# Weight sums of the column pairs by accumulating transfers, and retention steps one tick later

## The chip, the cores and the metric

The kernel runs on one core of a Trainium2 chip. The metric is the device time of one execution in microseconds (us), shown as the median of several runs. Each engine works through its own instruction list in order: TensorE (PE; its weight loads are shown as PEld), VectorE (DVE), ScalarE (ACT), GpSimd (POOL) and SyncE (SP), which issues the transfers. They meet through semaphores. A framework orders the instructions of each engine when the program is built, by dependencies, program order and its own estimates; on the chip the order is fixed.

## The reference

Two layers on x of 1024 tokens by 1024 channels, in float32. The change lies in the first, a retention layer:

```python
h = rmsnorm(x, g_pre)
proj = h @ w_in                                  # 1024 x 6144
q, k, v, gate = split(proj, [1024, 2048, 4096])
q = rope(q by 8 heads of 128); k = rope(k by 8 heads) * 128 ** -0.5; v by 8 heads of 256
# chunks of 64 tokens, per head:
scores = (q_i @ k_i.T) * inner_dec               # inside a chunk
cross  = (q_i @ R) * xi                          # from the state of the chunks before
R      = R * g_c + (k_i * zeta).T @ v_i
o = groupnorm(scores @ v_i + cross) * gn_gain
x = x + rmsnorm((silu(gate) * o) @ w_out, g_post)
```

The second layer is an attention over a shared compressed key and value (a gate projection, softmax over earlier chunks, an output projection); the change leaves its code as it is.

## The kernel before, in words

**Products.** A float32 matrix product is made of three matmuls on float32r parts: each operand is split into a high part (ScalarE, L238) and the rest (VectorE, L239), and `mm3` (L232 to L234) adds lo x hi, hi x lo and hi x hi. On top of that, the large products use Strassen's scheme in Winograd's form: seven half-size products in place of eight, with sums of blocks as operands.

**Column pairs.** In the first layer q, k and the gate are made in 16 column pairs, two for each of the eight heads: the q pair (columns of q and k) and the g pair (two gate columns). A pair is seven products, a to g (`pair`), each 12 matmuls of 128 x 512. The left operand of a product (its weights) is a "unit": half of a 128 x 1024 weight block, split in hi and lo. Three units are plain halves of the raw blocks r0 and r1 (`wraw`), four are sums T1 to T4 of such halves (`wsum`). Their making, in `make_sums`, is four subtractions on VectorE (L98, L99, L103, L104): T1 = r0 hi - r0 lo, T2 = r1 hi - T1, T3 = r1 hi - r0 hi, T4 = r1 lo - T2, where lo and hi are the column halves.

**When a unit is made.** `next` hands out a unit at the start of a product and prepares units until three are ready. It then sees to it that the pair after the next one is fetched: this falls at the start of product d of each pair, for the pair two further on. Buffers of 128 x 1024 come from one pool of 51 (`Heap`), first freed, first taken; a new writer waits for the last user of the buffer.

**Retention between the products.** After each product `tick` runs what is due of a list (`later`). When the last columns of q and k of a token half are there (half 1 after product f, half 0 after product g of the q pair), `rotate_a` applies the rope: two ScalarE copies of 64 x 1024 into xs (L656, L657), then three VectorE operations of 128 x 1024 (L660, L661, L662). From the end of the q pair, the four steps of each half are put on the list: scores (L693 transposes k, L699 multiplies q and k), values (the load `vt` is split), states (matmuls r<-v,z, then the state R is updated on VectorE, L755, and split), mix (matmuls r<-v,a and r<-r,q). The mix takes statistics on VectorE (L778, L779, L782), the power -0.5 on GpSimd (rg, L783) and nb on VectorE (L790). One product later ScalarE writes the normalized y (L793), and three products later TensorE transposes y (L810), VectorE multiplies by the gate (L813), and SyncE stores yT. The products at which these steps come are these numbers, counted from the end of the q pair:

```python
wait = (1, 2, 4, 6, 8, 9, 11, 13) if h < NH - 1 else (1, 2, 3, 5, 4, 6, 8, 10)
```

The first four are scores, values, states and mix of half 0, the others those of half 1. So half 0 comes in the head's g pair, half 1 in the q pair of the next head. The matmuls of these steps write PSUM tiles named r (four banks), those of the products tiles named acc (four banks).

Of the kernel before, what the change touches and what calls it, by code (L numbers as in the profile page):

```python
# [13 lines left out]
ALU = mybir.AluOpType  # L14
# [8 lines left out]
HALF = 512  # L23
HT = HALF // P
NT = S // P
NH = 8
# [6 lines left out]
class Heap:  # L33


    def __init__(self, pool, n):
        self.pool, self.n = pool, 0
        self.idle = deque(range(n))
        self.at = {}
# [13 lines left out]
class Units:  # L53
# [3 lines left out]

    def __init__(self, T, order, source, ahead, early=0):  # L60
        self.T, self.order, self.source, self.ahead, self.early = T, order, source, ahead, early
        self.at = self.n_fetched = 0
        self.pairs = list(dict.fromkeys(p for p, _ in order))
        self.raw, self.sums, self.made, self.left, self.ready = {}, {}, {}, {}, deque()

    def fetch(self):
        if self.n_fetched == len(self.pairs):
            return
        T, p = self.T, self.pairs[self.n_fetched]
        self.n_fetched += 1  # L70
        src, gains = self.source(p)
        self.raw[p] = [T.heap.get("wraw") for _ in range(2)]
        for j in range(2):
            r = self.raw[p][j]
            T.nc.sync.dma_start(r, src[j])
            if gains is not None:
                v = r.rearrange("p (n k c) -> p n k c", n=2, k=4)
                for k in range(4):
                    T.nc.scalar.activation(v[:, :, k, :], v[:, :, k, :], AF.Copy, scale=gains[:, 4 * j + k:4 * j + k + 1])  # L79
        self.left[p] = {"r0": 3, "r1": 5, "ta": 3, "tb": 3}  # L80

    def done(self, p, *names):
        left = self.left[p]
        for n in names:
            left[n] -= 1
            if not left[n]:
                self.T.heap.free(self.raw[p][int(n[1])] if n[0] == "r" else self.sums[p][n == "tb"])
# [110 lines left out]
class Trunk:  # L198
# [228 lines left out]
    def layer_a(self):  # L427
        nc, I, heap = self.nc, self.I, self.heap

        nc.scalar.activation(self.small([P, 1], "warm"), self.mhalf, AF.Silu)  # L430
        make_identity(nc, self.ident)
        self.X, A = {}, {}
        wide = WideUnits(self, NH // 4, lambda g, j, n, b: I["w_v"][g, j, n, b])
        rows = [[heap.get("xt") for _ in range(HT)] for _ in range(2)]
        for half in range(2):
            for t in range(HT):
                nc.sync.dma_start(rows[half][t], I["x"][half * HALF + t * P:half * HALF + (t + 1) * P, :])
                if half == 0 and t == 2:
                    wide.load(0)
            if half == 0:  # L440
                wide.load(1)
        self.first_rows(rows[0], A, wide)
        self.rows_norm(rows[1])
        for _ in self.rows_in(0, rows[0], A, ("A12",)):
            pass
        order = [(p, w) for p in range(2 * NH) for w in WINOGRAD]
        units = Units(self, order, lambda p: (I["w_in_a"][p], None), 3)
        self.values_a(wide, rows[1], A, units)
        sinks = [(h, kind) for h in range(NH) for kind in "qg"]
        self.heads = [{"h": h} for h in range(NH)]  # L450
        for p, (h, kind) in enumerate(sinks):
            if p == 2 * NH - 1:
                self.prepare_out_a()
            self.pair(units, getattr(self, "sink_" + kind)(h), over=p == 2 * NH - 1)
# [173 lines left out]
    def sink_q(self, h):  # L628

        st = self.heads[h]  # L630
        cb = {}

        def sink(i, j, bank, U):
            if i not in cb:
                cb[i] = [self.heap.get("qk"), 0]
            self.take(cb[i][0][:, j * HALF:(j + 1) * HALF], bank, U)
            cb[i][1] += 1
            if cb[i][1] == 2:
                st["qk", i] = cb[i][0]
                self.rotate_a(cb[i][0], i)  # L640
                if i == 0:
                    dm = st["dmask"] = self.small([P, P], "dm", bufs=2)
                    self.nc.sync.dma_start(dm, self.I["dmask"][:, h * P:(h + 1) * P])
                    wait = (1, 2, 4, 6, 8, 9, 11, 13) if h < NH - 1 else (1, 2, 3, 5, 4, 6, 8, 10)
                    steps = (self.ret_scores, self.ret_values, self.ret_states, self.ret_mix)
                    for n, (what, half) in zip(wait, [(w, i) for i in range(2) for w in steps]):
                        self.later(n, lambda what=what, half=half: what(st, half))
                    self.ret_load(st, 0)
                    self.later(wait[5] - 3, lambda: self.ret_load(st, 1))

        return sink
# [894 lines left out]
```

## Time and profile before

| | |
|---|---|
| median of 3 runs | 1268.6 us (1268.34 to 1268.72) |
| profiled execution | 1268.73 us |
| its span, first to last instruction | 1267.0 us |
| PE busy | 1240.5 us, 98% |
| DVE busy | 996.6 us, 79% |
| ACT busy | 639.6 us, 50% |
| POOL busy | 65.5 us, 5% |
| granted TensorE clock | 0.999 |

The profile is of one execution. A row of the groups reads: line, engine, operation, out<-in by the program's names, shape, count, then busy us, mean ns of one, and idle time of the engine before them with what ended it. A row of the timeline reads: start and duration in us, engine, line, operation, operands, count, and in brackets the idle time before it with its releaser. A matmul's duration includes the filling of the array, so matmuls overlap, and what one costs is the distance from its start to the next one's.

### The profile page before, as it was taken

How to read it: one execution, taken by the hardware profiler on the slowest of the kernel's cores; microseconds unless marked ns; L12 is line 12 of the kernel's file. 1: busy time of each engine (PE TensorE's matmuls, PEld its weight loads, DVE VectorE, ACT ScalarE, POOL GpSimd, SP SyncE). 2: the span in 40 equal slices, each digit the busy share in tenths (PEclk: the TensorE clock that was granted, in tenths of full speed). 3: DMA queues.
4: the chain of work that ended last, by engine and by line, in shares of the span. 5: the costliest groups of instructions: out<-in, count | busy, mean ns of one | idle time of the engine just before them, and what ended most of it. 6: DMA issues, size and time to landing. Idle time of an engine off the chain costs nothing. (4 is left out here: it accounts for less than half of the span.)

```text
span 1267.0 us, 17676 instructions
## 1 busy us (share of the span) xinstructions
PE 1240.5 (98%) x6568; PEld 1066.5 (84%) x6568; DVE 996.6 (79%) x1839; ACT 639.6 (50%) x1162; POOL 65.5 (5%) x86
## 2 busy tenths in 40 slices
PE   6999999999999999999999999999999999999997
PEld 5888878888888888888888789978898989898886
DVE  6888878898998998999966874675688788989622
ACT  7632125555564565565634875574445455456411
POOL 2000000000000000001000131200000000000000
PEclk9999999999999999999999999999999999999999
DMA  8248981232222322248663631124301020122321
GB/s 349 84 154 319 325 318 50 73 112 70 86 67 85 120 67 69 84 137 338 209 245 99 234 141 34 40 96 163 118 19 51 11 57 14 34 78 100 117 84 50
DMA packets 54166, 155.32 MB, mean 123 GB/s; under 512 B 6464, under 2 KB 15680, under 8 KB 54080
## 3 DMA queue, kind: packets, MB, share of 16 engines
q1 hardware_dynamic: 54080, 154.20, 34.9%
q8 instruction: 51, 0.84, 0.3%
q14 instruction: 35, 0.29, 0.1%
HBM read 113.28 MB, written 36.70 MB: 118 GB/s over the span
## 5 line engine op out<-in xcount | busy, mean ns | idle before, releaser
L232 PE MATMUL acc<-xhi,unit 128*128 128x512 f32 x560 | 220.6, 394 | 1.4 <-DVE unit L239 1.2
L233 PE MATMUL acc<-xlo,unit 128*128 128x512 f32 x560 | 219.2, 392 | 0.8 <-DVE xlo L239 0.8
L234 PE MATMUL acc<-xhi,unit 128*128 128x512 f32 x560 | 218.2, 390 | 0.0
L232 PEld LDWEIGHTS acc<-xhi,unit 128*128 128x128 f32 x560 | 105.3, 188 | 23.1 <-DVE unit L239 2.8
L234 PEld LDWEIGHTS acc<-xhi,unit 128*128 128x128 f32 x560 | 105.2, 188 | 21.7
L233 PEld LDWEIGHTS acc<-xlo,unit 128*128 128x128 f32 x560 | 105.4, 188 | 20.4 <-DVE xlo L239 1.1
L232 PE MATMUL acc<-vhi,xlo 128*128 128x512 f32 x224 | 89.3, 399 | 1.0 <-DVE xlo L239 1.0
L234 PE MATMUL acc<-vhi,xhi 128*128 128x512 f32 x224 | 88.4, 394 | 0.0
L233 PE MATMUL acc<-vlo,xhi 128*128 128x512 f32 x224 | 88.3, 394 | 0.0
L238 ACT ACTIVATE unit<-wsum 128x512 fp32r<-128x512 f32 x80 | 50.4, 631 | 59.9 <-PE acc L234 44.9
L1346 ACT ACTIVATE p<-S,nm 128x896 f32<-128x896 f32 (+3 forms) x64 | 47.4, 741 | 54.9 <-DVE nm L1343 50.2
L238 ACT ACTIVATE unit<-wraw 128x512 fp32r<-128x512 f32 x60 | 37.8, 630 | 53.6 <-issue 21.9
L238 ACT ACTIVATE pT<-r 128x512 fp32r<-128x512 f32 (+2 forms) x96 | 44.5, 489 | 37.8 <-PE r L1376 37.7
L238 ACT ACTIVATE vhi<-wv 128x1024 fp32r<-128x1024 f32 x28 | 29.3, 1060 | 64.4 <-PE acc L233 15.5
L239 DVE TENSOR_TENSOR unit<-wsum,unit 128x512 fp32r<-128x512 f32 x80 | 54.3, 684 | 8.5 <-ACT unit L238 8.2
L239 DVE TENSOR_TENSOR pT<-r,pT 128x512 fp32r<-128x512 f32 (+2 forms) x96 | 50.8, 549 | 4.8 <-ACT pT L238 4.5
L783 POOL TENSOR_TENSOR rg<-rg,mhalf 128x2 f32<-128x2 f32 x32 | 24.6, 769 | 548.2 <-DVE rg L782 528.0
L232 PEld LDWEIGHTS acc<-vhi,xlo 128*128 128x128 f32 x224 | 42.7, 191 | 10.1 <-DVE xlo L239 1.4
L232 PE MATMUL acc<-thi,slo 128*128 128x512 f32 x128 | 49.9, 393 | 0.6 <-DVE slo L239 0.6
L234 PEld LDWEIGHTS acc<-vhi,xhi 128*128 128x128 f32 x224 | 42.8, 191 | 9.1
L233 PEld LDWEIGHTS acc<-vlo,xhi 128*128 128x128 f32 x224 | 42.8, 191 | 8.7
L232 PE MATMUL acc<-whi,u 128*128 128x512 f32 x128 | 50.0, 391 | 0.0
(291 smaller groups left out, 3429.3 us busy)
## 6 DMA issues: line engine op xcount, KB each, us to landing
wraw<-in_w_in_a_dram SPq DMA_DIRECT2D x32, 512.0 KB, 4.1
wv<-in_w_v_dram SPq DMA_DIRECT2D x28, 512.0 KB, 6.3
wl<-in_w_out_a_dram SPq DMA_DIRECT2D x28, 512.0 KB, 6.0
yl<-yd SPq DMA_DIRECT2D x28, 512.0 KB, 4.8
vd<-vo SPq DMA_DIRECT2D x32, 256.0 KB, 2.9
td<-wl SPq DMA_DIRECT2D x16, 512.0 KB, 3.6
vt<-vd SPq DMA_DIRECT2D x16, 512.0 KB, 3.2
yd<-yT SPq DMA_DIRECT2D x16, 512.0 KB, 4.7
```

The source lines that it names most:

```text
L232: mm(ps, lhs[1], rhs[0], start=first, stop=False, skip_group_check=more)
L233: mm(ps, lhs[0], rhs[1], start=False, stop=False, skip_group_check=more)
L234: mm(ps, lhs[0], rhs[0], start=False, stop=last, skip_group_check=more)
L238: self.nc.scalar.activation(hi, src, AF.Copy)
L239: self.nc.vector.tensor_sub(lo, src, hi.bitcast(F32))
L783: nc.gpsimd.tensor_tensor(out=rg, in0=rg, in1=self.mhalf[:, 0:1].to_broadcast([P, 2]), op=ALU.pow)
L1346: nc.scalar.activation(p[:, :w].rearrange("p (a b) -> p a b", a=pieces), view, AF.Exp, bias=nm, accum_out=sm)
```

## The change

From the third column pair on, the four sums are no longer made by VectorE. At the fetch ScalarE writes -r0 into the buffer ta (128 x 1024) and -r1 hi into the second half of tb; SyncE copies r0 lo from DRAM into the first half of tb. Then three transfers issued by GpSimd add onto them: r0 hi and r1 hi onto the two halves of ta (T1 and T3), r1 lo onto the second half of tb, and, when all of these have landed, ta with its halves exchanged onto tb (T2 and T4). Besides, the retention steps of heads 0 to 6 come one product later.

```diff
@@ class Units
+    def __init__(self, T, order, source, ahead, early=0, queued=False):
...
+        self.queued = queued
@@ fetch
         self.left[p] = {"r0": 3, "r1": 5, "ta": 3, "tb": 3}
+        if self.queued and self.n_fetched > 2:
+            self.queue_sums(p, src)
+
+    def queue_sums(self, p, src):
+        T = self.T
+        nc = T.nc
+        ta, tb = self.sums[p] = [T.heap.get("wsum") for _ in range(2)]
+        lo, hi = slice(0, HALF), slice(HALF, 2 * HALF)
+        r0, r1 = self.raw[p]
+        two = lambda x: x.rearrange("p (j c) -> p j c", j=2)
+        onto = lambda o, i: nc.gpsimd.dma_start(o, i, accum_op=ALU.add)
+        nc.scalar.mul(ta, r0, -1.0)
+        nc.sync.dma_start(tb[:, lo], src[0][:, lo])
+        nc.scalar.mul(tb[:, hi], r1[:, hi], -1.0)
+        onto(two(ta), src.rearrange("j p c -> p j c")[:, :, hi])
+        onto(tb[:, hi], src[1][:, lo])
+        onto(two(tb), two(ta)[:, ::-1, :])
+        self.made[p] = {"T1", "T2", "T3", "T4"}
+        self.done(p, "r0", "r0", "r1", "r1", "r1", "ta", "tb")
@@ layer_a
-        units = Units(self, order, lambda p: (I["w_in_a"][p], None), 3)
+        units = Units(self, order, lambda p: (I["w_in_a"][p], None), 3, queued=True)
@@ sink_q
-                    wait = (1, 2, 4, 6, 8, 9, 11, 13) if h < NH - 1 else (1, 2, 3, 5, 4, 6, 8, 10)
+                    wait = (2, 3, 5, 7, 9, 10, 12, 14) if h < NH - 1 else (1, 2, 3, 5, 4, 6, 8, 10)
```

In the changed file later lines stand 21 lines further down (L238 becomes L259, L693 L714, L699 L720, L810 L831, L755 L776). Where rows move, three places in the middle of the stage (head 3).

TensorE in the g pair of head 3, at the scores of its half 0 (qk) and the transposes of the half 1 of the head before (y), before:

```order
L234 MATMUL acc_3298<-xhi_692,unit_3207 128x512
L232 MATMUL acc_3298<-xhi_692,unit_3207 128x512
L233 MATMUL acc_3298<-xlo_693,unit_3207 128x512
L234 MATMUL acc_3298<-xhi_692,unit_3207 128x512
L232 MATMUL acc_3298<-xhi_696,unit_3207 128x512
L693 MATMUL r_3227<-ident_120,qk_3095 128x128 x4
L699 MATMUL r_3234<-qk_3095 128x128 x4
L810 MATMUL r_3262<-ident_120,y_3118 128x128 x4
L810 MATMUL r_3268<-ident_120,y_3118 128x128 x4
L233 MATMUL acc_3298<-xlo_697,unit_3207 128x512
L234 MATMUL acc_3298<-xhi_696,unit_3207 128x512
L232 MATMUL acc_3298<-xhi_696,unit_3207 128x512
```

and now, where unit_3145 belongs to product c and unit_3219 to product d:

```order
L254 MATMUL acc_3282<-xlo_689,unit_3145 128x512
L255 MATMUL acc_3282<-xhi_688,unit_3145 128x512
L714 MATMUL r_3265<-ident_120,qk_3121 128x128 x4
L720 MATMUL r_3272<-qk_3121 128x128 x4
L253 MATMUL acc_3318<-xhi_692,unit_3219 128x512
L831 MATMUL r_3299<-ident_120,y_3160 128x128 x2
L254 MATMUL acc_3318<-xlo_693,unit_3219 128x512
L831 MATMUL r_3299<-ident_120,y_3160 128x128
L255 MATMUL acc_3318<-xhi_692,unit_3219 128x512
L831 MATMUL r_3299<-ident_120,y_3160 128x128
L831 MATMUL r_3305<-ident_120,y_3160 128x128 x4
```

The scores stood after 7 of the 12 matmuls of product d; they now stand ahead of it, right behind c, and the transposes of y are spread over d's first matmuls. The mix of the half 1 before them, which stood between products f and g of the q pair, now stands behind g.

The second place is the rotation just ahead of these scores. VectorE there, at the rotation of half 0 (the later qk and its xs) with what stands between, before:

```order
L662 TENSOR_TENSOR qk_3078<-qk_3078,xs_3166 128x1024
L782 TENSOR_SCALAR rg_3162<-mv_3155,ret_1513 128x2
L626 TENSOR_TENSOR qk_3095<-acc_3034,u_221_2979 128x512
L790 SCALAR_TENSOR_TENSOR nb_3191<-mv_3155,rg_3162 128x2
L239 TENSOR_TENSOR unit_3207<-wsum_3097,unit_3207 128x512
L239 TENSOR_TENSOR unit_3246<-wraw_2786,unit_3246 128x512
L660 TENSOR_TENSOR qk_3095<-qk_3095,cos_1515 128x1024
L661 TENSOR_TENSOR xs_3196<-xs_3196,sin_1516 128x1024
L406 TENSOR_TENSOR u_246_3243<-acc_3245,u_246_3243 128x512
L662 TENSOR_TENSOR qk_3095<-qk_3095,xs_3196 128x1024
```

and now (L681, L682, L683 are the rotation; unit_3145 and unit_3219 as above):

```order
L681 TENSOR_TENSOR qk_3121<-qk_3121,cos_1515 128x1024
L803 TENSOR_SCALAR rg_3181<-mv_3174,ret_1513 128x2
L260 TENSOR_TENSOR unit_3145<-wsum_2805,unit_3145 128x512
L800 BN_AGGR mv_3197<-st_3198 128x2
L799 BN_STATS st_3201<-r_3184 128x6
L682 TENSOR_TENSOR xs_3208<-xs_3208,sin_1516 128x1024
L800 BN_AGGR mv_3197<-st_3201 128x2
L260 TENSOR_TENSOR unit_3219<-wsum_2805,unit_3219 128x512
L803 TENSOR_SCALAR rg_3204<-mv_3197,ret_1513 128x2
L683 TENSOR_TENSOR qk_3121<-qk_3121,xs_3208 128x1024
L811 SCALAR_TENSOR_TENSOR nb_3234<-mv_3174,rg_3181 128x2
L811 SCALAR_TENSOR_TENSOR nb_3238<-mv_3197,rg_3204 128x2
```

The statistics and rg of the mix (L799, L800, L803) have come between the multiplies of the rotation, the sums of the units are gone from the list, and both nb now stand behind the last multiply. On ScalarE, correspondingly, the four y stood among the xs copies, and now stand behind the split of q that reads the rotated qk; before:

```order
L238 ACTIVATE unit_3207<-wsum_3097 128x512
L793 ACTIVATE y_3118<-r_3119,nb_3187,rg_3139 128x256 x2
L238 ACTIVATE unit_3246<-wraw_2786 128x512
L656 COPY xs_3196<-qk_3095 64x1024
L793 ACTIVATE y_3118<-r_3142,nb_3191,rg_3162 128x256 x2
L657 COPY xs_3196<-qk_3095 64x1024
L402 COPY u_246_3243<-acc_3206 128x512
L238 ACTIVATE unit_3281<-wsum_3098 128x512
L238 ACTIVATE q_360_3222<-qk_3095 128x512
```

and now, with the negations onto wsum (L96, L94) behind:

```order
L423 COPY u_244_3242<-acc_3218 128x512
L259 ACTIVATE vhi_3312<-vt_3216 128x1024
L259 ACTIVATE unit_3283<-wsum_2806 128x512
L259 ACTIVATE q_363_3260<-qk_3121 128x512
L814 ACTIVATE y_3160<-r_3161,nb_3234,rg_3181 128x256 x2
L814 ACTIVATE y_3160<-r_3184,nb_3238,rg_3204 128x256 x2
L264 ACTIVATE z_364_3263<-r_3265,ret_1513 128x512
L259 ACTIVATE a_365_3264<-a_366_3277 128x512
L259 ACTIVATE unit_3319<-wraw_2802 128x512
L96 ACTIVATE wsum_3327<-wraw_3323 128x512
L94 ACTIVATE wsum_3326<-wraw_3322 128x1024
```

The y rows have moved behind the split of qk, and two negations stand ahead of the splits of the next units. The third place is GpSimd's list in the middle of the stage; before, it held the powers of rg alone:

```order
L783 TENSOR_TENSOR rg_4173<-rg_4173,mhalf_121 128x2
L783 TENSOR_TENSOR rg_4196<-rg_4196,mhalf_121 128x2
L783 TENSOR_TENSOR rg_4438<-rg_4438,mhalf_121 128x2
L783 TENSOR_TENSOR rg_4461<-rg_4461,mhalf_121 128x2
L783 TENSOR_TENSOR rg_4690<-rg_4690,mhalf_121 128x2
```

and now, for two pairs:

```order
L93 DMA wsum_3060<-in_w_in_a_dram 128x2x512
L93 DMA wsum_3061<-in_w_in_a_dram 128x512
L93 DMA wsum_3061<-wsum_3060 128x2x512
L804 TENSOR_TENSOR rg_3181<-rg_3181,mhalf_121 128x2
L804 TENSOR_TENSOR rg_3204<-rg_3204,mhalf_121 128x2
L93 DMA wsum_3327<-in_w_in_a_dram 128x512
L93 DMA wsum_3326<-in_w_in_a_dram 128x2x512
L93 DMA wsum_3327<-wsum_3326 128x2x512
L804 TENSOR_TENSOR rg_3443<-rg_3443,mhalf_121 128x2
L804 TENSOR_TENSOR rg_3466<-rg_3466,mhalf_121 128x2
```

Three accumulating transfers stand ahead of each two powers, the third of them reading what the first wrote.

More of the change, by code (lines that the diff above doesn't have):

```diff
@@ L53 @@
 class Units:
-    def __init__(self, T, order, source, ahead, early=0):
+    def __init__(self, T, order, source, ahead, early=0, queued=False):
         self.T, self.order, self.source, self.ahead, self.early = T, order, source, ahead, early
+        self.queued = queued
         self.at = self.n_fetched = 0
```

## The prediction

> **What bounds the kernel now.** I read the page first, then the stage that the change touches, then what TensorE waits for there, then one head of it row by row.
>
> ```profile
> span 1267.0 us, 17676 instructions
> PE 1240.5 (98%) x6568; PEld 1066.5 (84%) x6568; DVE 996.6 (79%) x1839; ACT 639.6 (50%) x1162; POOL 65.5 (5%) x86
> ```
>
> TensorE is busy 98% of the span. The windows view (columns: window, then busy us of PE, PEld, DVE, ACT, POOL, granted clock, DMA share, GB/s) of 205 to 560 us, where the column pairs run, and TensorE's waits from 176 to 578 us (us in total, times, longest):
>
> ```profile
> 205.00:560.00 355.00, 354.51 (x1910) 304.62 (x1911) 320.44 (x629) 198.65 (x337) 21.05 (x28) 1.00 0.24 79
> PE acc L232 <- DVE unit L239: 1.2, 1, 1.2
> PE r L693 <- DVE qk L662: 0.4, 1, 0.4
> ```
>
> In 355 us TensorE is idle 0.49. VectorE is at 320.44 / 355 = 90%, which is much, but nobody pays for it. TensorE's matmuls overlap, though (0.39 long, started every 0.23), so short waits hide inside "busy"; they show as a late start. TensorE in head 3, from the last product matmul before the scores:
>
> ```profile
> 336.75 0.40 PE L232 MATMUL acc<-xhi,unit 128*128 128x512 f32 x1
> ...
> 342.22 0.28 PE L232 MATMUL r<-vhi,a 128*128 128x256 f32 x1
> ...
> 345.09 0.40 PE L232 MATMUL acc<-xhi,unit 128*128 128x512 f32 x1
> ...
> 347.84 0.39 PE L232 MATMUL acc<-xhi,unit 128*128 128x512 f32 x1
> ...
> 357.13 0.39 PE L234 MATMUL acc<-xhi,unit 128*128 128x512 f32 x1
> 357.36 0.39 PE L232 MATMUL acc<-xhi,unit 128*128 128x512 f32 x1
> 357.81 0.66 PE L693 MATMUL r<-ident,qk 128*128 128x128 f32 x4
> 358.31 1.06 PE L699 MATMUL r<-qk 128*128 128x128 f32 x8
> 359.20 1.04 PE L810 MATMUL r<-ident,y 128*128 128x128 f32 x8
> 359.99 0.47 PE L233 MATMUL acc<-xlo,unit 128*128 128x512 f32 x1
> ```
>
> One product takes 2.73 (two of them from 336.75 to 342.22), the mix 2.87 (342.22 to 345.09). L693 starts 0.45 after its predecessor instead of 0.23: 0.22 lost, to the last multiply of the rotation. It recurs once in each of the heads 1 to 7, as the row of the weight loader's waits has it (8 times; the first head's is the 0.4 above):
>
> ```profile
>   DVE qk L662: 3.8, 8
> ```
>
> So all that a lighter VectorE can give back here is 0.4 + 7 x 0.22 = 1.9 us, 0.15% of the span. The other 1.2 us fall before the changed pairs.
>
> **The change, part by part.**
>
> ```profile
> L98 DVE TENSOR_TENSOR wsum<-wraw 128x512 f32<-128x512 f32 x14 | 9.6, 683 | 0.5 <-DMA yd<-yT 0.5
> L238 ACT ACTIVATE vhi<-wv 128x1024 fp32r<-128x1024 f32 x28 | 29.3, 1060 | 64.4 <-PE acc L233 15.5
> L783 POOL TENSOR_TENSOR rg<-rg,mhalf x29: 689/692/973, 218.9 to 576.8; 128x2 f32<-128x2 f32 x29
> DMA to landing us min/median/max: 3.3/4.0/5.8
> wv<-in_w_v_dram SPq DMA_DIRECT2D x28, 512.0 KB, 6.3
> xt<-in_x_dram SPq DMA_DIRECT2D x8, 512.0 KB, 9.1
> ```
>
> Removed: 14 pairs x 4 subtractions of 0.68 (as L98) = 38 us of VectorE; its share falls to about 80%. Worth nothing in itself, since TensorE covers it.
>
> Added on ScalarE: 14 x (one negation of 1024 columns at 1.06 + one of 512 at about 0.6) = 23 us, on 198.65 of 355: 56% becomes 62%. Their duration is hidden; their wait need not be. Each stands in ScalarE's order and waits for the raw block, and behind it stand the splits of the next units and of the retention state R.
>
> Added on DMA: 1.5 MB a pair, 22 MB in 355 us, 62 GB/s beside 79. No row of before shows an accumulating transfer or one that GpSimd issues. Bounds: a plain one of the same 512 KB lands in 4.0 in this stage, and in 9.1 when sixteen queue up (xt). I take 5, nearer the first since the queues are a quarter full. GpSimd's queue then holds the third transfer until the first two have landed. Counted from the start of product d (where the fetch stands): the second raw block lands at 4, the negations end by 6, two issues of about 1, landing at 12, third issue done by 13. The next powers of rg behind it are wanted after product g, by VectorE's order not before 17. Even with 9.1 for 5 the third issue is over at 17. So this queue hides, and the shift by a tick (2.73) is what makes room: without it the powers would be due at 14.
>
> The sums are first used eleven products after the fetch, over 30 us; the chain of some 18 is hidden. Two buffers a pair are held from the fetch on; a unit's split may then have to wait for the product just finished, with three products (8.2 us) before it is used.
>
> The moved steps: each half's scores, values, states, mix, and with them its load of vt, the store of yT and the tail's transposes, come one product later. The vt load also moves one product later (it stays three ahead of its use), so its lead is unchanged; the store has whole pairs of time. SP's queue gets one more transfer a pair, behind the raw blocks; what stands behind it is a vt or a store.
>
> What decides is the new row order at the scores of half 0. The clock: 0 is the start of product f of the q pair, the first matmul after the states. TensorE wants L693 after f, g, the mix and a, b, c: 5 x 2.73 + 2.87 = 16.5. What must be ready is the rotation, on rows of before:
>
> ```profile
> 339.24 0.41 DVE L755 SCALAR_TENSOR_TENSOR R<-R,r 128x256 f32<-128x256 f32 x1
> ...
> 340.73 0.42 DVE L755 SCALAR_TENSOR_TENSOR R<-R,r 128x256 f32<-128x256 f32 x1
> ...
> 342.42 0.69 DVE L626 TENSOR_TENSOR qk<-acc,u 128x512 f32<-128x512 f32 x1 [0.36 <-PE acc L234]
> ...
> 346.48 0.76 DVE L778 BATCH_NORM_STATS2 st<-r 128x6 f32<-128x256 f32 x2
> 347.15 0.17 DVE L779 BATCH_NORM_AGGREGATE mv<-st 128x2 f32<-128x6 f32 x1
> 347.23 1.19 DVE L661 TENSOR_TENSOR xs<-xs,sin 128x1024 f32<-128x1024 f32 x1
> ...
> 348.47 1.22 DVE L662 TENSOR_TENSOR qk<-qk,xs 128x1024 f32<-128x1024 f32 x1
> 349.61 0.22 DVE L782 TENSOR_SCALAR rg<-mv,ret 128x2 f32<-128x2 f32 x1
> 349.74 0.69 DVE L626 TENSOR_TENSOR qk<-acc,u 128x512 f32<-128x512 f32 x1
> ...
> 350.81 0.69 DVE L239 TENSOR_TENSOR unit<-wsum,unit 128x512 fp32r<-128x512 f32 x1
> 351.41 0.68 DVE L239 TENSOR_TENSOR unit<-wraw,unit 128x512 fp32r<-128x512 f32 x1
> 356.54 1.22 DVE L662 TENSOR_TENSOR qk<-qk,xs 128x1024 f32<-128x1024 f32 x1
> 306.91 0.63 ACT L238 ACTIVATE q<-qk 128x512 fp32r<-128x512 f32 x1 [3.02 <-DVE qk L662]
> 307.45 1.04 ACT L238 ACTIVATE vhi<-vt 128x1024 fp32r<-128x1024 f32 x1
> ...
> 350.46 1.05 ACT L656 COPY xs<-qk 64x1024 f32<-64x1024 f32 x1
> 351.53 1.02 ACT L793 ACTIVATE y<-r,nb,rg 128x256 f32<-128x256 f32 x2
> ```
>
> From start to start: a step of R with its split 1.49 (339.24 to 340.73), a 1024-wide multiply 1.14 (348.47 to 349.61), a unit 0.60 (350.81 to 351.41), a pair of statistics 0.67, an aggregate 0.08, the small step of rg 0.13; on ScalarE a split of q 0.54 (306.91 to 307.45). In the new order VectorE makes three R updates (0.15 + 2 x 1.49 + 0.42, done at 3.5), the add behind f (to 4.1), then ScalarE two xs copies of 1.05 (to 6.3), and from 6.3 on VectorE never waits: six 1024-wide multiplies, four statistics, four aggregates, two rg steps, two units = 6 x 1.14 + 4 x 0.34 + 4 x 0.08 + 0.26 + 1.2 = 10.0. The last, whose row is 1.22 long, ends at 16.4. So L693 just makes it, 0.1 early instead of 0.22 late.
>
> Right behind, and this is new, stand the transposes L810 of y, whose four normalizations follow the split of q on ScalarE, and that waits for the same last multiply. Before, y was made in the middle of the rotation (351.53) and used at 359.20. Now: split from 16.4, 0.54; then four times 0.47 or so (two take 1.02 with their tail); y complete at 18.9, its first half at 18.0. TensorE wants the first at 16.5 + 1.39 (357.81 to 359.20) + 0.23 = 18.1 and the last 0.8 later, at 18.9. Just in time again, with nothing to spare.
>
> The sum: first head -0.4; heads 1 to 6 between -0.22 (all on time) and +0.6 (R done as late as before, 341.15 - 336.75 = 4.4 after the states, which delays all behind by 0.9, less 0.1 of slack and the 0.22). I take -0.12 each, since the chain closes on its rows but without margin: -0.7. Head 7 keeps its ticks: 0. Together -1.1 on the profiled execution's 1268.73, 1267.6; that execution stands 0.1 above the median, so about 1267.5. A difference under 0.2% (2.5 us) can't be told from none here, and the whole gain to be had is under it.
>
> **The rivals.**
> - *ScalarE led by the second raw block (slower).* Before its splits of R in product f, ScalarE negates the second raw block, issued when product c ends. A landing of 4.0 leaves about 1 us. But the first accumulating transfer, a store and the 256 KB copy now run beside it; with the 6.3 of wv the chain is 0.9 late: 6 x (0.9 - 0.22) - 0.4 = +3.7, 1272.3; with 7, 1276. It decides from about 6.1 on. Against it: the maximum so far is 5.8.
> - *GpSimd and VectorE in each other's way (slower).* Building descriptors is work on GpSimd. The nearest row is its power, 0.69 to 0.97. If one such issue stops VectorE within the chain, L693 and y are 0.9 late: +3.7, 1272.3 too. The Trainium skill (SBUF — State Buffer, "Who interferes with whom") says that VectorE's two-port modes and GpSimd shut each other out, that a two-input tensor_tensor collides only with GpSimd's reads, and infers that descriptors need writes; by that, this chain of two-input operations is spared, and the rows above are almost all of that kind. No row of before shows such an issue.
> - *More than the waits goes.* For over 2.5 us something outside the stage must gain; nothing in the profile speaks for it.
>
> **How the numbers follow.** On time or nearly (1266.4 to 1270.5): 0.58. Raw block late (1270.5 to 1276): 0.24. GpSimd in the way (1271 to 1278): 0.10. Gain over 2.5: 0.06. The rest, something untold: 0.02. Slower by over 0.2% (above 1271.1): nearly all of the second and third, 0.32; faster 0.06; same 0.62. The range, 1266.3 to 1273.5, leaves out the far ends of the second and third and the last gain; the likeliest case's own is 1266.4 to 1270.5.
>
> **What would show it.** Right: TensorE still idle under 1 us in this stage, VectorE near 80%, L693 without a late start, L810 within 0.3 of its place, POOL's rg waiting for VectorE, not for a transfer. Wrong: a late start of L810 or L693 of over 0.5 a head; ScalarE idle before the negation on wraw; a raw block landing in over 6; rg led by the third transfer.

## The result, and the profile after

The changed kernel takes 1291.3 us (median of 6 runs, 1288.6 to 1292.6), the kernel before 1268.7 in the same comparison: a ratio of 1.0176, 95% interval 1.0163 to 1.0189. It is 22.7 us slower, outside the predicted range. The profiled execution took 1288.6 us, and all comparisons of rows below are with it. The top of its page:

```profile
span 1286.8 us, 17842 instructions
PE 1246.7 (97%) x6568; PEld 1067.8 (83%) x6568; DVE 964.1 (75%) x1783; ACT 664.7 (52%) x1190; POOL 119.2 (9%) x128
```

The windows view of the stage of the column pairs (window, then busy us of PE, PEld, DVE, ACT, POOL, granted clock, DMA share, GB/s):

```profile
205.00:560.00 355.00, 340.00 (x1799) 288.27 (x1799) 271.46 (x539) 207.61 (x342) 69.01 (x65) 0.99 0.56 135
```

TensorE's waits from 200 to 560 us (us in total, times, longest):

```profile
PE acc L253 <- DVE unit L260: 13.0, 6, 2.4
PE r L714 <- DVE qk L683: 1.8, 4, 0.5
```

VectorE is relieved (76% of the stage instead of 90%), and yet TensorE, idle for 0.49 us of the stage before, is idle for 15.0 now: 13.0 in six waits for a unit, and 1.8 for the rotation right behind them. The timeline of TensorE at one of them, head 2's (start, us, engine, line, operation; in brackets the idle time before it and its releaser):

```profile
303.65 0.39 PE L255 MATMUL acc<-xhi,unit 128*128 128x512 f32 x1
306.19 0.50 PE L253 MATMUL acc<-xhi,unit 128*128 128x512 f32 x1 [2.15 <-DVE unit L260]
...
308.82 0.39 PE L255 MATMUL acc<-xhi,unit 128*128 128x512 f32 x1
309.65 0.66 PE L714 MATMUL r<-ident,qk 128*128 128x128 f32 x4 [0.45 <-DVE qk L683]
```

It recurs once a head in the heads 1 to 6, just before the scores of half 0. Followed back, the timeline of VectorE and then of ScalarE ahead of that wait:

```profile
292.89 0.69 DVE L260 TENSOR_TENSOR unit<-wraw,unit 128x512 fp32r<-128x512 f32 x1 [5.42 <-ACT unit L259]
293.50 0.41 DVE L776 SCALAR_TENSOR_TENSOR R<-R,r 128x256 f32<-128x256 f32 x1
...
296.45 0.42 DVE L776 SCALAR_TENSOR_TENSOR R<-R,r 128x256 f32<-128x256 f32 x1
...
305.44 0.69 DVE L260 TENSOR_TENSOR unit<-wsum,unit 128x512 fp32r<-128x512 f32 x1
287.12 0.63 ACT L96 ACTIVATE wsum<-wraw 128x512 f32<-128x512 f32 x1 [0.71 <-DMA wraw<-in_w_in_a_dram]
292.23 0.63 ACT L259 ACTIVATE unit<-wraw 128x512 fp32r<-128x512 f32 x1 [4.47 <-DMA yd<-yT]
...
294.10 0.42 ACT L259 ACTIVATE r<-R 128x256 fp32r<-128x256 f32 x1
```

TensorE waits until 306.19 for the unit whose low part VectorE makes at 305.44, in the middle of the rotation. The rotation is late since the three updates of R run only from 293.50 to 296.9, while TensorE began product f at 290.07; they stand on VectorE behind the low part of a unit of the g pair, and that waits for its high part on ScalarE, which stood still for 4.47 us until 292.23. What it waits for is a store, yd<-yT: the unit's buffer was yT's. Nobody was waiting for the stored y itself; the unit only wants the room. The timeline of GpSimd and SyncE (SPq is the queue of SyncE's transfers) shows when the store was issued, and what ahead of it:

```profile
282.30 1.23 POOL L93 DMA_DIRECT2D wsum<-in_w_in_a_dram  x1 [4.97 <-ACT wsum L94]
283.77 0.33 SPq L95 DMA_DIRECT2D wsum<-in_w_in_a_dram  x1
285.39 0.33 SPq L837 DMA_DIRECT2D yd<-yT  x1
```

And the list of the transfers issued from 275 to 300 us (size, us from issue to landing):

```profile
wsum<-in_w_in_a_dram POOLq DMA_DIRECT2D x1, 512.0 KB, 8.4
wraw<-in_w_in_a_dram SPq DMA_DIRECT2D x1, 512.0 KB, 4.2
yd<-yT SPq DMA_DIRECT2D x1, 512.0 KB, 6.8
wsum<-in_w_in_a_dram SPq DMA_DIRECT2D x1, 256.0 KB, 7.1
```

The first accumulating transfer of the new pair started 3.1 us ahead of the store and needed 8.4 us; beside it the 256 KB copy took 7.1 and the store 6.8. 285.39 + 6.8 = 292.2, which is where ScalarE goes on.

In the kernel before, the same store was not quick either. Its row from 275 to 300 us, and ScalarE's wait for such stores from 200 to 560 us:

```profile
yd<-yT SPq DMA_DIRECT2D x1, 512.0 KB, 5.2
ACT unit L238 <- DMA yd<-yT: 3.6, 5, 0.9
```

It stood behind two raw blocks and landed in 4.5 to 5.2 in heads 1 to 6, but the unit that got its buffer came later, so ScalarE waited 0.9 at most.

One more loss hangs on TensorE's waits. After two of the six (heads 3 and 4), its matmuls start about 427 ns apart instead of 227 for a while; here in head 3:

```profile
359.79 0.69 PE L253 MATMUL acc<-xhi,unit 128*128 128x512 f32 x1 [1.89 <-DVE unit L260]
360.28 0.63 PE L254 MATMUL acc<-xlo,unit 128*128 128x512 f32 x1
360.70 0.63 PE L255 MATMUL acc<-xhi,unit 128*128 128x512 f32 x1
361.13 0.63 PE L253 MATMUL acc<-xhi,unit 128*128 128x512 f32 x1
```

The windows view of this stretch has the granted clock in its third column from the end:

```profile
360.00:366.00 6.00, 6.00 (x28) 4.93 (x27) 5.47 (x12) 3.40 (x7) 1.86 (x2) 0.72 0.12 18
```

It is 0.72 over these 6 us, so the stretch costs 0.28 x 6 = 1.7 us; in head 4, from 414 to 420 us, it is 0.72 as well. The Trainium skill (TensorE: Matmul & The Clock Gate, "Part 1: The HAM clock gate") has the array fall to half its clock after an idle window of about 3.4 us and gives 426.7 ns for 512 columns then. The pitch agrees; here idle times of 1.9 and 2.1 us were followed by the slow stretch, in two of six cases.

The sum closes: take, from 200 to 575 us, the time by which the matmul behind one of 512 columns starts later than 227 ns after it. It adds up to 25.6 us after and 5.8 before; the difference, 19.8, is that of the two spans (1286.8 - 1267.0). The two slow stretches are 3.4 of it.

### The profile page after: what moved, and what is told of

Same layout as the page of the kernel before. It is cut to its first block, busy times and chain, and to the rows that moved or that the text cites. A ratio compares the mean times of both kernels' runs of the same rounds, so it can differ in the third digit from the quotient of the medians.

```text
span 1286.8 us, 17842 instructions
## 1 busy us (share of the span) xinstructions
PE 1246.7 (97%) x6568; PEld 1067.8 (83%) x6568; DVE 964.1 (75%) x1783; ACT 664.7 (52%) x1190; POOL 119.2 (9%) x128
## 3 DMA queue, kind: packets, MB, share of 16 engines
q0 software_dynamic: 9632, 18.35, 8.6%
## 5 line engine op out<-in xcount | busy, mean ns | idle before, releaser
L253 PE MATMUL acc<-xhi,unit 128*128 128x512 f32 x560 | 223.7, 399 | 14.0 <-DVE unit L260 13.9
L255 PE MATMUL acc<-xhi,unit 128*128 128x512 f32 x560 | 219.9, 393 | 0.0
L259 ACT ACTIVATE unit<-wraw 128x512 fp32r<-128x512 f32 x60 | 37.8, 630 | 64.8 <-DMA yd<-yT 27.2
L259 ACT ACTIVATE unit<-wsum 128x512 fp32r<-128x512 f32 x80 | 50.0, 627 | 40.4 <-issue 16.7
L260 DVE TENSOR_TENSOR unit<-wraw,unit 128x512 fp32r<-128x512 f32 x60 | 41.2, 689 | 38.8 <-ACT unit L259 38.7
L259 ACT ACTIVATE pT<-r 128x512 fp32r<-128x512 f32 (+2 forms) x96 | 44.6, 489 | 38.1 <-PE r L1397 37.9
L260 DVE TENSOR_TENSOR unit<-wsum,unit 128x512 fp32r<-128x512 f32 x80 | 54.5, 686 | 10.8 <-ACT unit L259 10.3
L259 ACT ACTIVATE vhi<-wv 128x1024 fp32r<-128x1024 f32 x28 | 29.3, 1061 | 63.4 <-PE acc L254 15.6
L93 POOL DMA_DIRECT2D wsum<-in_w_in_a_dram x28 | 30.2, 1094 | 276.1 <-DMA wsum<-in_w_in_a_dram 168.8
```

Of the source, the lines that this page charges most:

```text
L93: onto = lambda o, i: nc.gpsimd.dma_start(o, i, accum_op=ALU.add)
L253: mm(ps, lhs[1], rhs[0], start=first, stop=False, skip_group_check=more)
L255: mm(ps, lhs[0], rhs[0], start=False, stop=last, skip_group_check=more)
L259: self.nc.scalar.activation(hi, src, AF.Copy)
L260: self.nc.vector.tensor_sub(lo, src, hi.bitcast(F32))
```

## The experiments

Ratios are against the kernel before, on the same chip.

**First theory: the buffers.** Before, the buffer of half 0's yT went to a unit made two products after the store. With two sum buffers taken at the fetch, the pool (first freed, first taken) hands it out one product earlier. Four kernels, one comparison (the kernel before: 1268.3 us). The ticks alone:

```diff
-        units = Units(self, order, lambda p: (I["w_in_a"][p], None), 3, queued=True)
+        units = Units(self, order, lambda p: (I["w_in_a"][p], None), 3)
```

> The shifted ticks alone; the sums are VectorE's as before. Theory (buffers): the loss of 22.7 us is a unit's split on ScalarE that waits for the store of yT, because the early hold of two sum buffers hands yT's buffer to that unit one product after the store instead of two. Without the early hold the next holder of yT's buffer comes two products later again: 1266 to 1270 us, no wait of a unit for yd<-yT over 1 us. Rival (ticks): the later steps squeeze the rotation and y: 1285 to 1292 us. Rival (transfers): 1266 to 1270 us too.

Measured: 1271.9 us, ratio 1.0030 [1.0020, 1.0041]. This kernel is 3.5 us slower, not 23. Even that isn't the price of the ticks alone: here a sum buffer is the one that follows yT, and VectorE's subtraction waits for the store, 10.8 us in six times; the third kernel (the hold alone) has the same ticks and loses nothing.

The queued sums alone:

```diff
-                    wait = (2, 3, 5, 7, 9, 10, 12, 14) if h < NH - 1 else (1, 2, 3, 5, 4, 6, 8, 10)
+                    wait = (1, 2, 4, 6, 8, 9, 11, 13) if h < NH - 1 else (1, 2, 3, 5, 4, 6, 8, 10)
```

> The queued sums alone, with the ticks of before. Now the buffer of yT goes, one product after its store, not to a unit but to a sum buffer taken at the fetch. Buffers: the negation into it and the copy into it wait for the store instead, some 2 to 4 us later than a unit would have wanted it, so part of the loss goes: 1269 to 1282 us. Ticks: 1266 to 1270 us. Transfers (accumulating transfers and negations cost it by themselves): 1285 to 1292 us.

Measured: 1314.5 us, 1.0361 [1.0346, 1.0377], worse than every theory had it. VectorE's longest wait in it, in total, from 200 to 590 us:

```profile
DVE nb L811 <- POOL rg L804: 57.5, 26, 6.1
```

Without the shift the powers of rg stand in GpSimd's queue behind the third transfer, which waits for the first two. That is a loss of its own, which the shift removes.

The hold alone, with shifted ticks:

```diff
         ta, tb = self.sums[p] = [T.heap.get("wsum") for _ in range(2)]
...
-        nc.scalar.mul(ta, r0, -1.0)
-        nc.sync.dma_start(tb[:, lo], src[0][:, lo])
-        nc.scalar.mul(tb[:, hi], r1[:, hi], -1.0)
-        onto(two(ta), src.rearrange("j p c -> p j c")[:, :, hi])
-        onto(tb[:, hi], src[1][:, lo])
-        onto(two(tb), two(ta)[:, ::-1, :])
-        self.made[p] = {"T1", "T2", "T3", "T4"}
-        self.done(p, "r0", "r0", "r1", "r1", "r1", "ta", "tb")
...
-            ta, tb = self.sums[p] = [T.heap.get("wsum") for _ in range(2)]
+            if p not in self.sums:
+                self.sums[p] = [T.heap.get("wsum") for _ in range(2)]
+            ta, tb = self.sums[p]
```

> Shifted ticks; the two sum buffers are taken at the fetch as in the changed kernel (so every block goes to the same holder as there), but VectorE makes the sums later as before: no negation, no accumulating transfer. Buffers: the unit still waits for the store, which lands in about 5 us as before instead of 6.8: 2 to 3 us a head in six heads, 1276 to 1288 us. Transfers: 1266 to 1270 us. Ticks: 1285 to 1292 us.

Measured: 1268.2 us, 0.9998 [0.9988, 1.0008]. The buffer of half 0's yT goes to the same unit as in the changed kernel, one product after the store, and nothing is lost. So the first theory is not enough. ScalarE's wait for the store (200 to 590 us), and the landing of the yT stores from 190 to 560 us:

```profile
ACT unit L252 <- DMA yd<-yT: 12.9, 7, 3.2
DMA to landing us min/median/max: 2.6/2.6/4.1
```

The unit does wait for the store, but the store lands in 2.6 or 2.7 us in most heads, and TensorE does not feel it.

The changed kernel with yT's buffer returned two products later:

```diff
             nc.sync.dma_start(self.yd[h][half], yT)
-            heap.free(yT)
+            self.later(2, lambda: heap.free(yT))
```

> The changed kernel, with yT's buffer given back to the pool two products after its store instead of at once; nothing else differs. Buffers: the unit gets another buffer, its wait for yd<-yT (28 us in seven times) goes, and TensorE's 13.9 us wait for the unit with it: 1266 to 1271 us, granted clock back to 1.00. Ticks, transfers, and a slow second raw block: all of the loss stays, 1285 to 1292 us.

Measured: 1294.1 us, 1.0202 [1.0182, 1.0222]. By the expectation this speaks against the buffers altogether. The trace shows why it doesn't decide. The timeline of ScalarE and of SyncE:

```profile
288.39 0.40 ACT L259 ACTIVATE r<-R 128x256 fp32r<-128x256 f32 x1
292.80 0.63 ACT L259 ACTIVATE unit<-wsum 128x512 fp32r<-128x512 f32 x1 [4.01 <-issue]
286.63 0.33 SPq L837 DMA_DIRECT2D yd<-yT  x1
```

The store in its list of transfers from 275 to 300 us:

```profile
yd<-yT SPq DMA_DIRECT2D x1, 512.0 KB, 6.1
```

286.63 + 6.1 = 292.7. The profile names no releaser for this wait (of the six in heads 1 to 6 it names the store for one), but each of the six, 3.9 to 5.9 us long, ends within 0.1 us of the store's landing: ScalarE waits for the same store, one unit later. With yT's buffer held back, the pool is used up by the unit that takes it (all 51 buffers held), so whoever comes last gets yT's; two products on, that is the next unit, in almost the same place.

**Second theory: crowding.** The hold makes a unit depend on the store, and the accumulating transfers make the store late; it takes both. Four kernels (the kernel before: 1268.8 us), in which yT's buffer goes where it goes in the changed kernel unless said otherwise (some other buffers change hands, contrary to what the expectation says). First, only every second pair's sums are queued, and the hold stays for all; the kernel after it has `!= 0` in place of `!= 1`:

```diff
         ta, tb = self.sums[p] = [T.heap.get("wsum") for _ in range(2)]
+        if p % 2 != 1:
+            return
...
```

VectorE makes the other pairs' sums later, as before.

> Shifted ticks and the early hold for all pairs, but the queued sums only for the g pairs (fetched away from the store of half 0); the q pairs' sums are VectorE's. Every block has the holder that it has in the changed kernel. Theory now (crowding): the queued transfers of the q pair are in the rings when half 0's yT is stored, the store takes 6.8 us instead of 2.6, and the unit that took over yT's buffer leads ScalarE 4.5 us late; neither the hold nor the ticks cost anything by themselves. Without the q pairs' transfers the store lands in 2.6 to 3.5: 1265 to 1270 us. Rival (negations and queued sums cost time wherever they are): half of the loss, about 1280 us.

Measured: 1269.1 us, 1.0006 [0.9997, 1.0015].

> The mirror: the queued sums only for the q pairs, the hold for all, VectorE making the g pairs' sums. Crowding: all of the loss stays, and VectorE is fuller: 1287 to 1296 us, half 0's store at 6 to 8 us. Rival (cost wherever they are): about 1280 us.

Measured: 1288.6 us, 1.0160 [1.0143, 1.0177]. The g pairs' transfers cost next to nothing, the q pairs' 19.8 us: the cost isn't in the sums but in where they fall. ScalarE's waits for the store (200 to 560 us), first with the g pairs' sums queued, then with the q pairs':

```profile
ACT unit L263 <- DMA yd<-yT: 12.6, 7, 2.4
```

```profile
ACT unit L263 <- DMA yd<-yT: 25.4, 6, 5.1
```

The store of half 0 issued from 275 to 300 us lands in 2.7 us in the first and in 6.8 in the second. Waits of up to 2.4 us hardly cost TensorE anything (with the hold alone one of 3.2 cost nothing either); waits of 4 to 5 do.

The changed kernel with the q pairs' sums two products later:

```diff
         if self.queued and self.n_fetched > 2:
-            self.queue_sums(p, src)
+            k = 2 if p % 2 == 0 else 0
+            T.later(k, lambda: self.queue_sums(p, src)) if k else self.queue_sums(p, src)
```

> The changed kernel, with the q pairs' sum buffers taken, and their negations and transfers started, two products later; the store of half 0 then goes ahead of the copy and of the accumulating transfers, and yT's buffer goes to a state block two products after the store. Crowding: the wait of ScalarE for yd<-yT goes, 1265 to 1271 us. Rival (cost wherever they are): 1280 to 1292 us. Rival (GpSimd's queue): the third transfer's issue comes 5 us later and the powers of rg wait for it: over 1275 us.

Measured: 1267.3 us, 0.9991 [0.9981, 1.0000]. The windows view of the stage:

```profile
205.00:560.00 355.00, 355.00 (x1920) 305.02 (x1918) 288.56 (x572) 222.41 (x366) 71.40 (x67) 1.00 0.57 140
```

The store of half 0 in the list of transfers from 275 to 300 us:

```profile
yd<-yT SPq DMA_DIRECT2D x1, 512.0 KB, 2.6
```

TensorE is busy for all of the 355 us. The store leaves ahead of the copy and of the accumulating transfers, and the wait for it is gone. Since the sum buffers are taken later too, half 0's yT buffer now goes to a block of the state; so this kernel changes both the crowding and the holder, and doesn't tell one from the other.

Plain transfers at the same places (this kernel leaves out the adding, so its sums are not the sums):

```diff
-        onto = lambda o, i: nc.gpsimd.dma_start(o, i, accum_op=ALU.add)
+        onto = lambda o, i: nc.gpsimd.dma_start(o, i)
```

> The changed kernel with the three transfers of GpSimd written plainly instead of accumulated (so the sums of the column pairs are wrong), at the same places and of the same sizes. If adding in the transfer is what makes them slow, the store of half 0 lands in about 4 us instead of 6.8 and most of the loss goes: 1266 to 1276 us. If the bytes in the rings do it, whoever adds: 1284 to 1292 us. A plain 512 KB of GpSimd would land in 4 us by the first, in 6 or more by the second.

Measured: 1281.6 us, 1.0104 [1.0089, 1.0119], between the two cases. GpSimd's queue over the whole span, on the page of the changed kernel and then of this one (packets, MB, share of the 16 DMA engines):

```profile
q0 software_dynamic: 9632, 18.35, 8.6%
```

```profile
q0 software_dynamic: 5152, 18.35, 4.4%
```

This kernel's list of transfers from 275 to 300 us, to be held against the 8.4, 4.2 and 6.8 above:

```profile
wsum<-in_w_in_a_dram POOLq DMA_DIRECT2D x1, 512.0 KB, 6.2
wraw<-in_w_in_a_dram SPq DMA_DIRECT2D x1, 512.0 KB, 5.5
yd<-yT SPq DMA_DIRECT2D x1, 512.0 KB, 5.0
wsum<-wsum POOLq DMA_DIRECT2D x1, 512.0 KB, 3.1
```

Adding in the transfer nearly doubles packets and engine time for the same bytes. Without it about 10 us (of 22.7) come back. That is only in part the store: it is 1.8 us faster here, but over heads 1 to 6 it lands in 5.0 to 6.5 instead of 6.1 to 7.9, 0.8 less in the mean. ScalarE's wait for it is 8.8 us in seven times instead of 27.2 in six, and the granted clock stays at 1. What is left comes in part another way: the second raw block now takes 5.5, and ScalarE's negation waits for it (17.2 us in six times).

**What carries the loss, and what doesn't** (the kernel before: 1268.1 us). The changed kernel with yT's buffer given back one product after the store, all transfers as crowded:

```diff
-            heap.free(yT)
+            self.later(1, lambda: heap.free(yT))
```

> The changed kernel with yT's buffer given back one product after its store. All transfers stay as crowded (store of half 0 lands in 6.8), but the buffer now goes to the second state block, which ScalarE wants only at its third split of R, about 3 us after the unit. Crowding through the buffer: ScalarE's wait for the store shrinks from 4.5 to about 1.5 us a head, and half to three quarters of the loss go: 1273 to 1281 us. If the crowded rings hurt in another way (second raw block, queue of GpSimd), it stays at 1285 to 1292 us.

Measured: 1270.8 us, 1.0020 [1.0011, 1.0029]. The store of half 0 takes 6.9 us, as slow as ever, but its buffer went to the second state block; ScalarE's timeline:

```profile
290.67 0.42 ACT L259 ACTIVATE r<-R 128x256 fp32r<-128x256 f32 x1 [1.40 <-DMA yd<-yT]
```

The wait of 1.4 is what was expected, the time is better than expected: about 20 of 22.7 us come back from one delayed line, with the transfers as crowded. So the slow store does its damage through the buffer that it holds. Part of the 2.7 us that stay is one late raw block: in head 6 it landed in 7.9, ScalarE's negation waited 4.4 for it, and TensorE then waited 1.0 for a unit, its one such wait.

The negations alone:

```diff
         nc.scalar.mul(ta, r0, -1.0)
-        nc.sync.dma_start(tb[:, lo], src[0][:, lo])
         nc.scalar.mul(tb[:, hi], r1[:, hi], -1.0)
-        onto(two(ta), src.rearrange("j p c -> p j c")[:, :, hi])
-        onto(tb[:, hi], src[1][:, lo])
-        onto(two(tb), two(ta)[:, ::-1, :])
-        self.made[p] = {"T1", "T2", "T3", "T4"}
...
```

The hold stays, and VectorE makes the sums later, over the negated values.

> Shifted ticks, early hold, ScalarE's two negations of each pair at their places, but no copy and no accumulating transfer; VectorE makes the sums afterwards as before, over the negated values. It prices the negations on ScalarE and their wait for the raw blocks alone. Crowding: they cost next to nothing, 1266 to 1270 us. ScalarE led by the second raw block: 1272 to 1285 us.

Measured: 1268.1 us, 1.0001 [0.9991, 1.0010]. ScalarE's 23 us are hidden, and so is their wait for the raw blocks when these land on time.

The version with the q pairs' sums two products later, once more:

> The version with the q pairs' negations and transfers two products later, again and with more rounds: is it ahead of the kernel before? TensorE waits for nothing in this stage in its trace, so the 1.9 us that the waits before were worth are gained, nothing else: 1266.5 to 1268, ratio 0.998 to 0.9995. Chance alone: ratio 1.000.

Measured: 1267.3 us, 0.9991 [0.9982, 1.0000]. Both comparisons put it about 1 us ahead of the kernel before, and both intervals end at 1.000. That is the size of the removed waits, but just at the edge of what can be told from none.

## Why the prediction was wrong, point by point

- *What VectorE's relief is worth.* Right. TensorE had 1.9 us of waits for VectorE to lose in this stage, and the version in which nothing new waits is 1.5 and 0.8 us ahead, at the edge of the noise.
- *ScalarE's 23 us hidden.* Right, by the negations alone.
- *The accumulating transfer at 5 us, between 4.0 and 9.1.* Taken too low: in the changed kernel the 36 of them from 220 to 545 us land in 4.7 to 9.5. The upper bound was nearly the right one.
- *GpSimd's queue hides it, and the shift makes the room.* Right in both halves. In the changed kernel the powers wait for VectorE (POOL rg L804 <- DVE rg L803), not for a transfer, and without the shift they do wait, with the kernel 46 us slower than before.
- *The clock of R, rotation and y.* It closes where its start is on time: in the version with the later q sums R is done 3.2 us after the states (head 2), and TensorE waits neither for the rotation nor for y. In the changed kernel its first term failed: the updates of R, expected to be done 3.5 us after the states, began behind the stalled unit and were done 6.8 after (290.07 to 296.87). TensorE lost 2.9 in that head, 2.3 ahead of the unit and 0.6 ahead of the scores.
- *The step that failed* is the sentence on the two buffers: "a unit's split may then have to wait for the product just finished, with three products (8.2 us) before it is used". It looked for the last user among matmuls. The last user was a store, and the 8.2 us were the unit's own, while behind the unit on ScalarE stood the splits of R. A wait ahead of these of up to 2.4 us was seen to cost next to nothing (once one of 3.2); here it was 4.1 to 5.5. Its companion, "the store has whole pairs of time", asked when the stored data are read, not when the buffer is wanted. And of the transfers beside the new ones only the raw block was priced, not the store: where the new transfers were out of its way it landed in 2.6, here in 6.8.
- *The rivals.* A slow second raw block: it took 4.2, below the 6.1 from which it was to decide; it led only with plain transfers, and in one head of the kernel with the delayed `free`. GpSimd and VectorE in each other's way: not seen. With all issues in their places the kernel with the delayed `free` takes 1270.8 us, and in the changed kernel the low parts of units from raw blocks take 0.69 us on VectorE whether an issue runs beside them or not. The forecast had a rival of the right sign and of another mechanism, at a sixth of the size.
- *Not settled:* the profiled execution is 2.8 us below the median of its kernel. The runs differ in granted clock (0.991 to 0.997, the profiled one at 0.997), which would fit slow stretches after more of the six waits, but only one execution was read row by row.

## What to carry to other kernels

When buffers come from a shared pool, ask of each new hold who gets the next buffers, who used them last, and when that use ends; a store is a user until it lands, whoever reads the data. When transfers are added, price the ones that run beside them, above all a store whose buffer is wanted next, and let that store go first. A freed engine is worth only the waits that it caused; here that was 1.9 us, and one misplaced wait of 4.5 us a head cost twelve times as much.

## What was not expected of the hardware

- A transfer that adds onto its target takes about twice the packets and DMA time of a plain one (9632 and 8.6% against 5152 and 4.4% for 18.35 MB). The last transfer of a q pair, with little beside it, landed in 5.0 us accumulating and 3.1 plain. For 512 KB the formula of the Trainium skill (DMA: Bandwidth & Descriptors, "Anatomy of one DMA", 2.0 us plus bytes / 436,000) gives an estimate of 3.2: the plain one agrees, the accumulating one does not.
- A plain transfer's landing depends on what was issued shortly before it. The 512 KB store of half 0 (heads 1 to 6) took 2.6 to 4.1 us with the hold alone (in head 2 a raw block was issued 2.4 us ahead of it), 4.5 to 5.2 behind two raw blocks, 5.0 to 6.5 behind a raw block, the copy and a plain transfer of GpSimd, and 6.1 to 7.9 where that one adds. The 256 KB copy took 7.1 in head 2's q pair, and about 3.3 in the g pairs, where it goes ahead of the accumulating transfers. The same page of the Trainium skill ("Queues, rings and completion order") has each DMA engine take turns between queues packet by packet, which fits, though no run here shows the turns themselves.
- TensorE's clock fell after 1.9 and 2.1 us of idle time, and did not after others of 2.1 and 2.4.
